# A hybrid decoder block on one core: pace of the attention, order of the loads at the border of the output projection, and its weights asked a unit ahead

## The chip, the core and the metric

The kernel runs on one core of a Trainium2 chip. Five engines work side by side, each through its own queue in order: TensorE (PE in the profile, its weight loads PEld), VectorE (DVE), ScalarE (ACT), GpSimd (POOL) and SyncE (SP, whose queue SPq issues nearly all transfers here; 16 DMA engines carry them out). They wait for one another through semaphores. The metric is the device time of one execution in microseconds (us).

## What is computed

The reference is one layer over x of 2048 positions by 1024 channels:

```python
h = rmsnorm(x, norm1_g[l])
proj = h @ w_in[l]
p_q, p_k, p_v, p_g, p_a, c_b, c_c, c_h = jnp.split(proj, splits, axis=-1)
...
o = gla_chunked(q, k, v, log_a)
o = rmsnorm(o, gla_norm_g[l]).astype(x.dtype)
o = o * jax.nn.silu(p_g.reshape(bsz, seq, GLA_HEADS, GLA_DV))
...
o_conv = c_b * causal_depthwise_conv(u, conv_w[l])
mixed = jnp.concatenate([o_gla, o_conv], axis=-1) @ w_out[l]
x = x + mixed
h2 = rmsnorm(x, norm2_g[l])
ffn = (jax.nn.silu(h2 @ w_ffn_gate[l]) * (h2 @ w_ffn_up[l])) @ w_ffn_down[l]
x = x + ffn
```

and a last RMSNorm. The attention is gated linear attention in chunks with a state that is carried from chunk to chunk; the convolution part takes 512 of the 1024 columns that the output projection mixes.

## The kernel before

**Products.** Every matrix is float32 and is split in two numbers of a shorter format, a high and a low one (`split`, L195: ScalarE rounds to the high part, L198; VectorE subtracts it to get the low part, L199). A product of two tiles is then three matmuls: high by high, high by low, low by high (`product_step`, L496 to L498). The large multiplications are done in units of 2 x 2 blocks by a scheme that needs seven products instead of eight. `PRODUCTS` (L38) lists their operands: weights A11, S1, S2, A12, S3, S4, A22, and inputs B11, T1, T2, B21, T3, B22, T4, in this order. A unit's seven results are added up by VectorE (L530; at the border L1351) or copied out by ScalarE (L542).

**Whole operands and pairs.** Input operands lie in DRAM either as a pair (high and low, 512 KB) or, for T3, B22 and T4 (`WHOLE`, L47), whole (256 KB), so that they have to be split once they are loaded. `load_undivided` loads a whole one, `load_pair` a pair; both take a buffer of the pool `opp`, which has 28. In a unit the whole ones are split when they fall due (`due`, L580): T3 behind the fourth product's sum, and so on.

**Order of work.** The 2048 positions are four blocks of 512, done in two halves of two blocks. Second half's input projection (`in_proj(1, ops)`, L1834) is 12 units: keys and queries, values (units 0 to 3), gate (units 4 and 5, with a silu on ScalarE, L597), convolution (units 6 to 11). Then comes the border: the first half's output projection, `first_out_proj` (L1331), in four units d0 = 0, 2, 4, 6. Each has seven convolution products of six matmuls (operands of `mix_operands`) and 48 matmuls on the attention's heads (L1383, L1389), and each loads 1 MB of `wout` into one of two `raw` buffers. Then `out_proj` (L1421 to L1424) does the second half with plain products, first the convolution's channels, then the heads; the feed-forward part follows.

**Attention in the background.** `gla_half` is a generator whose steps are put between the products. Of three steps to a chunk one does scores (L1170) and transposes (L1176, L1179), one turns the chunk before around (L1245) and asks the next chunk's 14 small loads, and one, the output step, does the outputs (L1195, L1202), the state (L1210), the root mean square of each head (L1227 squares, L204 logarithm, L205 exponential) and the scaled result `osb` (L1236). `tick` (L276) is called after each product; a unit has seven ticks, a unit of the border eight. Every second tick takes one step of the background. While `hasty` holds, the odd tick whose count leaves 3 on division by four takes one too, so three ticks in four; `hastened(steps, n)` sets that and ends it at step n. Other odd ticks advance the making of the convolution operands (`ahead`). In the second input projection the background is a pause of three steps, then `gate(1)` (5 steps) with `gla_half(0)` (27 steps) under `hastened(..., 26)`, and behind it, under `hastened(..., 9)`, `gla_half(1)` of the same length, which runs on into the border.

**Queues.** The order in which each engine gets its instructions is fixed when the program is built, by a list scheduler: of the instructions that it thinks ready, it takes the one first written. So a load or a split can be issued well ahead of its place in the code, once its buffer is thought free. `behind(marks)` (L163) queues what it holds behind the marks on the marks' engine alone: behind a sum it holds back VectorE's half of a split and not ScalarE's.

The functions that the change touches and what calls them:

Of the kernel before, what the change touches and what calls it, by code (L numbers as in the profile page):

```python
# [20 lines left out]
P = 128  # L21
# [33 lines left out]
def tile_hymba_block(ctx, tc, x, xt, win, wa, wgu, wout, wffn, wdown, wdown_first, small, out):  # L55
# [106 lines left out]
    @contextmanager  # L162
    def behind(marks):  # L163

        with ExitStack() as stack:
            for m in marks:
                stack.enter_context(tc.issue_after(m.ins))
            yield
# [134 lines left out]
    def pause(n):  # L303
        for _ in range(n):
            yield

    def hastened(steps, n):
        hasty.append(True)
        for i, _ in enumerate(steps):
            if i == n:  # L310
                hasty.clear()
            yield
# [17 lines left out]
    def no_operands():  # L330
        return {b: [] for _, b in PRODUCTS}
# [88 lines left out]
    def raw_weights(src):  # L420
        n = src.shape[-1]
        raw = rawp.tile([P, 4 * PB], F32, name="raw", tag="raw")[:, 0 : 4 * n]
        raw = raw.rearrange("p (a n) -> p a n", a=4)
        raw_loads.append(load(raw, src))
        return raw
# [154 lines left out]
    def due(n):  # L580
        for o in undivided.pop(n, ()):
            with behind(last_out):
                split(o[:, 1, :].bitcast(F32), o[:, 0, :], o[:, 1, :])
# [398 lines left out]
    def load_undivided(src):  # L982
        o = opp.tile([P, 2, PB], F32R, name="op", tag="op")
        load(o[:, 1, :].bitcast(F32), src[:])
        return o
# [7 lines left out]
    def load_pair(src):  # L993
        o = opp.tile([P, 2, PB], F32R, name="op", tag="op")
        load(o[:].bitcast(F32), src[:])
        return o
# [11 lines left out]
    def gate(half, ops, mark=None):  # L1008

        a = bank("a_ps")
        names = "B11", "T1", "B21", "B22"
        with behind([mark] if mark else []):
            for n in names:
                for k in range(4):
                    q = {"B11": 3 * k + 1, "T1": 3 * k, "B21": 2 * k + 13, "B22": 2 * k + 12}[n]
                    w = wa_sb[:, 32 * q : 32 * q + P]
                    for e in range(2):
                        pe.matmul(  # L1020
                            a[:], w, ops[n][k][:, e, :],
                            start=(n, k, e) == ("B11", 0, 0),
                            stop=n == "B22" and k == 3 and e == 1, skip_group_check=True,
                        )
        if mark:
            yield

        stacks = []
        if half == 0:
            second_factor()  # L1030
        for j in range(2):
            stack = bx[0].tile([96, PB], F32R, name="a_sb", tag="b")
            r, low = [slice(32 * n, 32 * n + 32) for n in (j, 1 - j)]
            with behind(held):
                act.activation(stack[r, :], a[r, :], AF.Copy)
                act.activation(stack[64:96, :], a[r, :], AF.Copy)
                dve.tensor_tensor(stack[low, :], a[r, :], stack[r, :].bitcast(F32), ALU.subtract)
            stacks.append(stack)
        yield
        for j in range(2):  # L1040
            small = decays[2 * half + j] = [
                mtiny.tile([P, 2, PT], F32, name=n, tag=n, bufs=4) for n in ("em", "dn", "el")
            ]
            for i in range(2):
                z = bank("z")
                pe.matmul(
                    z[:], wgu_sb[:, i * P : (i + 1) * P], stacks[j][:], start=True, stop=True
                )
                forget_gate(2 * half + j, i, z, *small)
                yield  # L1050
# [69 lines left out]
    def gla_half(half):  # L1120
        chunks = [(b, t) for b in (2 * half, 2 * half + 1) for t in range(PT)]
        with tc.issue_after(last_silu[0].ins):
            tables = act.preload_act_table_set("natural_log_exp_and_others")
        fetched = gla_fetch(*chunks[0])
        yield
        with tc.issue_after(tables.ins):
            cur = gla_scaled(*fetched)
        yield
        o = None
        for n, (b, t) in enumerate(chunks):  # L1130
            s = gla_scores(b, t, *cur)
            yield
            if n + 1 < len(chunks):
                fetched = gla_fetch(*chunks[n + 1])
            if o is not None:
                yield from gla_finish(*chunks[n - 1], *o)
            o = gla_outputs(b, t, *s)
            if n + 1 < len(chunks):
                cur = gla_scaled(*fetched)
            yield  # L1140
        yield from gla_finish(b, t, *o)
        done.add((b, t))
        yield
# [166 lines left out]
    def mix_operands():  # L1310
        for _ in ahead.pop():
            pass
        s_conv["B22"] = s_mix[1][2:4]
        ops = no_operands()
        for _, n in PRODUCTS:
            ops[n] = [(load_undivided if n in WHOLE else load_pair)(p) for p in s_conv[n]]
            if n in WHOLE:
                undivided[n] = ops[n]
        return ops, [[load_pair(s_gla[j][:, k]) for j in range(2)] for k in range(HEADS)]

    def residual(d0):
# [9 lines left out]
    def first_out_proj(y, conv, heads):  # L1331

        ssq = [
            tiny.tile([P, PB], F32, name=f"ssx{j}", tag=f"ssx{j}", bufs=1) for j in range(2)
        ]
        for d0 in range(0, KD, 2):
            raw = raw_weights(wout[d0 // 2]).rearrange("p a (b e c) -> p (a b) e c", e=2, c=P)
            quads = [raw[:, k : k + 2, e, :] for e, k in ((0, 4), (0, 6), (1, 6), (1, 4))]
            w = unit_weights(None, quads)
            wh = [weight_quarter(raw[:, 0:HEADS, e, :]) for e in range(2)]  # L1340

            def mul(i, o=None):
                first = o is None
                o = bank() if first else o
                n, m = PRODUCTS[i]
                for k in range(2):
                    product_step(o, w[n], conv[m], k, first)
                return o

            def plus(at, o):  # L1350
                summed = dve.tensor_tensor(y[at][:], o[:], y[at][:], ALU.add)  # L1351
                all_plus.append(summed)
                if d0 == 0:
                    last_plus[:] = last_out[:] = [summed]

            oa = mul(0)
            plus((0, 0), oa)
            ob = mul(1)
            plus((1, 1), ob)
            due("T3")  # L1360
            tick()
            mul(2, oa)
            plus((0, 1), oa)
            due("B22")
            o = mul(3)
            tick()
            mul(4, oa)
            plus((1, 1), oa)
            due("T4")
            mul(5, ob)  # L1370
            plus((0, 1), ob)
            tick()
            mul(6, oa)
            plus((1, 0), oa)
            tick()
            following = residual(d0 + 2) if d0 + 2 < KD else None
            for e in range(2):
                po = [bank() if e or j else o for j in range(2)]
                for k in range(HEADS):
                    c = slice(k * P, (k + 1) * P)  # L1380
                    for j in range(2):
                        for part in range(2):
                            pe.matmul(  # L1383
                                po[j][:], wh[e][:, 0, c], heads[k][j][:, part, :],
                                start=k + part == 0 and e + j > 0, stop=False,
                                skip_group_check=True,
                            )
                    for j in range(2):
                        pe.matmul(  # L1389
                            po[j][:], wh[e][:, 1, c], heads[k][j][:, 0, :], start=False,  # L1390
                            stop=k == HEADS - 1, skip_group_check=True,
                        )
                    if k % 2:
                        tick()
                for j in range(2):
                    plus((e, j), po[j])
                    store(s_x1[j][d0 + e][:], y[e, j][:])
                    sum_squares(ssq[j], y[e, j][:], d0 + e == 0)
            y = following
        return ssq  # L1400
# [429 lines left out]
    drain_background()  # L1830
    ops = load_pairs(s_h1)
    ahead.append(conv_operands())
    background.extend([pause(3), hastened(chain(gate(1, ops), gla_half(0)), 26)])
    in_proj(1, ops)  # L1834
    drain_background(lambda: (1, PT - 1) in done)
    ssq = first_out_proj(residual(0), *mix_operands())
# [118 lines left out]
```

## Time and profile before

| what | value |
|---|---|
| median of 3 runs | 2037.68 us (2036.74 to 2039.19) |
| the profiled execution's own time | 2035.8 us |
| its span, first instruction to last | 2034.0 us |
| granted clock of TensorE over the span | 0.997 |
| HBM read, written | 277.60 MB, 145.75 MB |
| DMA, mean over the span | 209 GB/s |

In a row of the timeline stand the start and the duration in us, engine, line, operation, what it writes and reads, and how many instructions are taken together; in brackets how long the engine had been idle and what ended that. Matmuls are pipelined: one of 512 columns shows some 0.39 us, and its successor starts earlier than that. Each row of a table by stage has the stretch and its length, the busy time of PE, PEld, DVE, ACT and POOL with the number of instructions, the granted clock, the busy share of the DMA engines and GB/s.

### The profile page before, as it was taken

The numbers are of one execution on the slowest core, as the hardware profiler recorded it, in microseconds if no ns is written. First come the engines' busy times: TensorE is split into PE (matmuls) and PEld (weight loads), VectorE is DVE, ScalarE is ACT, GpSimd is POOL, SyncE is SP. The second block draws the span as 40 slices with busy tenths as digits, with TensorE's granted clock in tenths as the row PEclk, the third lists the DMA queues.
The fourth block names the chain that finished last, engine by engine and source line by source line (L and its number), as shares of the span: only waits on it lengthen the run. The fifth ranks groups of instructions, "written<-read, shape, count | busy, mean of one in ns | idle before, by whom it ended". The sixth has DMA issues, their size and how long they took to land.

```text
span 2034.0 us, 27037 instructions
## 1 busy us (share of the span) xinstructions
PE 2010.5 (99%) x9275; PEld 1653.5 (81%) x9275; DVE 1566.8 (77%) x2837; ACT 978.3 (48%) x1944; POOL 10.3 (1%) x17
## 2 busy tenths in 40 slices
PE   9999999999999999999999999999999999999998
PEld 8788887778878888888888888887888888888886
DVE  7888868678767877777777688887767767778886
ACT  6664465765543444444444552334434444454345
POOL 0000000000000000000000000000000000000001
PEclk9999999999999999999999999999999999999999
DMA  7356866655596863446545676576444434586653
GB/s 264 120 201 219 289 261 214 192 177 176 183 318 227 281 244 135 182 153 214 181 150 186 225 282 252 185 278 275 167 158 171 169 137 171 179 332 219 248 217 130
DMA packets 193482, 425.16 MB, mean 209 GB/s; under 512 B 20320, under 2 KB 67648, under 8 KB 183872
## 3 DMA queue, kind: packets, MB, share of 16 engines
q1 hardware_dynamic: 192624, 422.77, 58.7%
q8 instruction: 73, 1.20, 0.2%
q10 hardware_dynamic: 720, 0.66, 0.1%
q14 instruction: 65, 0.53, 0.1%
HBM read 277.60 MB, written 145.75 MB: 208 GB/s over the span
## 4 chain that ended last, share of the span: by engine, by line
PE 92%; DMA 3%; DVE 2%; ACT 2%; issue 1%; SPq 1%; POOL 0%; POOLq 0%; ACTq 0%; DVEq 0%
PE mm L496 27%; PE mm L498 27%; PE mm L497 26%; PE mm L1422 1%; PE mm L1424 1%; PE mm L1421 1%; PE mm L1383 1%; DMA op<-shT 1%; PE a_ps L1020 1%; PE mm L801 1%; PE mm L803 1%; PE mm L802 1%; PE mm L1741 1%; PE mm L1389 1%; DMA raw<-in_win_dram 1%
## 5 line engine op out<-in xcount | busy, mean ns | idle before, releaser
L496 PE MATMUL mm<-op,wq 128*128 128x512 f32 x2499 | 973.0, 392 | 5.2 <-DVE osb L1236 2.0
L497 PE MATMUL mm<-op,wq 128*128 128x512 f32 x2499 | 972.2, 390 | 0.3 <-DVE op L199 0.2
L498 PE MATMUL mm<-op,wq 128*128 128x512 f32 x2499 | 962.0, 390 | 2.4 <-DVE wq L199 2.1
L198 ACT ACTIVATE wq<-raw 128x512 fp32r<-128x512 f32 (+2 forms) x628 | 361.2, 581 | 601.0 <-PE mm L498 497.2
L496 PEld LDWEIGHTS mm<-op,wq 128*128 128x128 f32 x2499 | 469.3, 188 | 108.0 <-ACT wq L198 2.9
L498 PEld LDWEIGHTS mm<-op,wq 128*128 128x128 f32 x2499 | 469.3, 188 | 102.5 <-DVE wq L199 4.4
L497 PEld LDWEIGHTS mm<-op,wq 128*128 128x128 f32 x2499 | 469.5, 188 | 98.1 <-DVE op L199 2.0
L199 DVE TENSOR_TENSOR wq<-raw,wq 128x512 fp32r<-128x512 f32 (+2 forms) x628 | 390.5, 627 | 149.3 <-ACT wq L198 147.6
L530 DVE TENSOR_TENSOR c<-mm,c 128x512 f32<-128x512 f32 x196 | 134.9, 688 | 71.5 <-PE mm L498 66.8
L530 DVE TENSOR_TENSOR y<-mm,y 128x512 f32<-128x512 f32 x185 | 126.9, 689 | 53.5 <-PE mm L498 52.9
L542 ACT ACTIVATE c<-mm 128x512 f32<-128x512 f32 x198 | 115.7, 589 | 32.4 <-PE mm L498 29.8
L448 DVE TENSOR_TENSOR raw<-raw 128x512 f32<-128x512 f32 (+2 forms) x190 | 116.8, 621 | 2.1
L198 ACT ACTIVATE wq<-s 128x512 fp32r<-128x512 f32 (+2 forms) x100 | 58.0, 580 | 106.8 <-PE mm L498 93.7
L448 DVE TENSOR_TENSOR s<-raw 128x512 f32<-128x512 f32 (+2 forms) x95 | 59.1, 622 | 33.4 <-DMA raw<-in_wffn_dram 18.0
L199 DVE TENSOR_TENSOR op<-op 128x512 fp32r<-128x512 f32 x108 | 71.2, 686 | 1.8 <-ACT op L198 1.7
L198 ACT ACTIVATE op<-op 128x512 fp32r<-128x512 f32 x108 | 63.1, 621 | 14.2 <-DMA op<-scT 7.0
L199 DVE TENSOR_TENSOR wq<-s,wq 128x512 fp32r<-128x512 f32 (+2 forms) x100 | 62.5, 625 | 1.8 <-ACT wq L198 1.0
L448 DVE TENSOR_TENSOR raw<-s,raw 128x512 f32<-128x512 f32 (+2 forms) x95 | 59.1, 622 | 1.3
L597 ACT ACTIVATE sg<-mm 128x512 f32<-128x512 f32 x26 | 15.6, 598 | 87.6 <-PE mm L498 87.6
L597 ACT ACTIVATE c<-c 128x512 f32<-128x512 f32 x78 | 49.0, 629 | 15.4 <-DVE c L530 12.7
L1421 PE MATMUL mm<-op,wq 128*128 128x512 f32 x128 | 50.2, 392 | 0.0
L1422 PE MATMUL mm<-op,wq 128*128 128x512 f32 x128 | 49.8, 389 | 0.0
(238 smaller groups left out, 1664.5 us busy)
## 6 DMA issues: line engine op xcount, KB each, us to landing
raw<-in_wffn_dram SPq DMA_DIRECT2D x44, 1024.0 KB, 6.4
sa_B<-so SPq DMA_DIRECT2D x47, 512.0 KB, 4.2
op<-sa_B SPq DMA_DIRECT2D x47, 512.0 KB, 6.7
raw<-in_win_dram SPq DMA_DIRECT2D x22, 1024.0 KB, 5.9
sa_T<-so SPq DMA_DIRECT2D x44, 512.0 KB, 4.5
op<-sa_T SPq DMA_DIRECT2D x44, 512.0 KB, 6.4
raw<-in_wdown_dram SPq DMA_DIRECT2D x24, 768.0 KB, 5.4
sx<-y SPq DMA_DIRECT2D x48, 256.0 KB, 4.2
```

The costliest lines, as they stand in the source:

```text
L198: last_hi[:] = [act.activation(hi, src, AF.Copy)]
L199: last_lo[:] = [dve.tensor_tensor(lo, src, hi.bitcast(F32), ALU.subtract)]
L448: dve.tensor_tensor(*args)
L496: pe.matmul(o[:], wh, xh, start=first and k == 0, stop=False, skip_group_check=True)
L497: pe.matmul(o[:], wh, xl, start=False, stop=False, skip_group_check=True)
L498: return pe.matmul(o[:], wl, xh, start=False, stop=k == n - 1, skip_group_check=True)
L530: last_plus[:] = [dve.tensor_tensor(t[:], o[:], t[:], ALU.add)]
L542: last_out[:] = [act.activation(t[:], o[:], AF.Copy)]
L597: last_silu[:] = [act.activation(s[:], c[:], AF.Silu)]
L801: pe.matmul(acc[:], wq[:, 0, c], p[:, 0, :], start=first, stop=False)
L1421: pe.matmul(o[e, j][:], wh, m[:, 0, :], start=n == 0, stop=False)
L1422: pe.matmul(o[e, j][:], wh, m[:, 1, :], start=False, stop=False)
```

## The change

In `mix_operands` the three whole convolution operands (two tiles each) are loaded ahead of the four pairs, and their splits are written there, VectorE's halves behind the last sum of the input projection; the three `due` calls in `first_out_proj` go. In `first_out_proj` the weights of unit d0 + 2 are asked before those of unit d0 are split. And the first attention's hastened stretch ends at step 12 instead of 26.

```diff
         ops = no_operands()
+        for n in WHOLE:
+            ops[n] = [load_undivided(p) for p in s_conv[n]]
         for _, n in PRODUCTS:
-            ops[n] = [(load_undivided if n in WHOLE else load_pair)(p) for p in s_conv[n]]
-            if n in WHOLE:
-                undivided[n] = ops[n]
+            if n not in WHOLE:
+                ops[n] = [load_pair(p) for p in s_conv[n]]
+        with behind(last_plus):
+            for n in WHOLE:
+                for o in ops[n]:
+                    split(o[:, 1, :].bitcast(F32), o[:, 0, :], o[:, 1, :])
         return ops, [[load_pair(s_gla[j][:, k]) for j in range(2)] for k in range(HEADS)]
...
+        raws = raw_weights(wout[0])
         for d0 in range(0, KD, 2):
-            raw = raw_weights(wout[d0 // 2]).rearrange("p a (b e c) -> p (a b) e c", e=2, c=P)
+            raw, raws = raws, raw_weights(wout[d0 // 2 + 1]) if d0 + 2 < KD else None
+            raw = raw.rearrange("p a (b e c) -> p (a b) e c", e=2, c=P)
...
             plus((1, 1), ob)
-            due("T3")
             tick()
             mul(2, oa)
             plus((0, 1), oa)
-            due("B22")
             o = mul(3)
             tick()
             mul(4, oa)
             plus((1, 1), oa)
-            due("T4")
...
-    background.extend([pause(3), hastened(chain(gate(1, ops), gla_half(0)), 26)])
+    background.extend([pause(3), hastened(chain(gate(1, ops), gla_half(0)), 12)])
```

## The prediction

> **What bounds the kernel now.** I read the page first, then a table by stage of the half that the change touches, then the idle times of TensorE in order of time.
>
> ```profile
> span 2034.0 us, 27037 instructions
> PE 2010.5 (99%) x9275; PEld 1653.5 (81%) x9275; DVE 1566.8 (77%) x2837; ACT 978.3 (48%) x1944; POOL 10.3 (1%) x17
> ```
>
> TensorE is busy 2010.5 of 2034.0 us. The change neither adds nor removes a matmul, so it can only win or lose idle time: 23.5 us in the whole kernel, plus what a lower clock costs. The table by stage (stretch, length and then busy time of PE, PEld, DVE, ACT and POOL, granted clock, DMA share, GB/s) shows where. The rows are the two gate units of the second input projection, its other units, and the four units of the first output projection (d0 = 0, 2, 4, 6).
>
> ```profile
> 373.00:420.00 47.00, 43.48 (x259) 34.87 (x259) 29.82 (x65) 39.86 (x75) 0.00 (x0) 1.00 0.59 186
> 420.00:537.00 117.00, 116.84 (x636) 94.65 (x635) 89.58 (x190) 63.74 (x169) 0.00 (x0) 1.00 0.50 157
> 563.00:595.00 32.00, 29.35 (x148) 22.42 (x146) 17.32 (x42) 11.20 (x37) 0.00 (x0) 0.95 0.89 317
> 595.00:619.00 24.00, 22.87 (x112) 18.49 (x112) 21.69 (x51) 14.23 (x39) 0.00 (x0) 1.00 0.80 283
> 619.00:640.00 21.00, 21.00 (x94) 17.41 (x93) 13.73 (x27) 6.31 (x13) 0.00 (x0) 1.00 0.48 162
> 640.00:660.50 20.50, 20.50 (x92) 16.95 (x92) 14.71 (x25) 7.16 (x12) 0.00 (x0) 1.00 0.89 319
> ```
>
> Idle TensorE: 47.00 - 43.48 = 3.5 us in the gate units, 2.65 at d0 = 0, 1.1 at d0 = 2, nothing later. Its rows in order of time name the releaser:
>
> ```profile
> 315.52 0.50 PE L498 MATMUL mm<-op,wq 128*128 128x512 f32 x1 [2.14 <-DVE wq L199]
> 391.54 0.47 PE L496 MATMUL mm<-op,wq 128*128 128x512 f32 x1 [1.67 <-DVE osb L1236]
> 408.64 0.63 PE L1179 MATMUL v_ps<-ident,vt 128*128 128x128 f32 x4 [1.84 <-ACT wq L198]
> 570.25 0.41 PE L1176 MATMUL kt_ps<-ident,kq 128*128 128x128 f32 x2 [2.19 <-ACT wq L198]
> 571.69 0.80 PE L496 MATMUL mm<-op,wq 128*128 128x512 f32 x1 [0.46 <-DVE y L1351]
> 595.38 0.47 PE L496 MATMUL mm<-op,wq 128*128 128x512 f32 x1 [0.28 <-DVE osb L1236]
> 600.67 1.16 PE L1195 MATMUL o_ps<-vt,scores 128*128 128x128 f32 x8 [0.35 <-ACT vt L1181]
> 602.97 0.50 PE L496 MATMUL mm<-op,wq 128*128 128x512 f32 x1 [0.49 <-DVE y L1351]
> ```
>
> The largest is that at the border, 570.25. The timeline of all engines just ahead of it tells its cause:
>
> ```profile
> 560.53 0.38 SPq L152 DMA_DIRECT2D op<-scT  x1
> 561.49 0.38 SPq L152 DMA_DIRECT2D op<-scT  x1
> 565.82 0.63 ACT L198 ACTIVATE op<-op 128x512 fp32r<-128x512 f32 x1 [4.88 <-DMA op<-scT]
> 567.10 0.63 ACT L198 ACTIVATE op<-op 128x512 fp32r<-128x512 f32 x1
> 567.34 0.71 PE L1170 MATMUL sc<-kq 64*128 64x128 f32 x8
> 568.41 0.17 DVE L1230 TENSOR_SCALAR hsq<-hsq 128x4 f32<-128x4 f32 x1 [5.24 <-ACT sq L1227]
> 569.68 0.76 DVE L1236 TENSOR_TENSOR osb<-o_ps,hsq 128x256 f32<-128x256 f32 x2
> ```
>
> The last two whole operands (T4) are asked at 560.53 and 561.49. ScalarE's queue is in order: with the split of T4 at its head it stands 4.88 us until the first has landed. The squares of the attention's outputs stand behind it, so VectorE stands 5.24 us, so the accumulators are emptied late, and TensorE has no free bank until `osb` is made at 569.68 and after. This one late load holds three engines. The clock falls after it; two matmuls ahead of it and two behind it, and the granted clock (last but two column) of the stretch:
>
> ```profile
> 563.17 0.39 PE L498 MATMUL mm<-op,wq 128*128 128x512 f32 x1
> 563.40 0.39 PE L496 MATMUL mm<-op,wq 128*128 128x512 f32 x1
> ...
> 572.28 0.63 PE L497 MATMUL mm<-op,wq 128*128 128x512 f32 x1
> 572.71 0.63 PE L498 MATMUL mm<-op,wq 128*128 128x512 f32 x1
> ```
>
> ```profile
> 570.00:575.00 5.00, 4.29 (x18) 3.29 (x18) 5.00 (x12) 1.55 (x4) 0.00 (x0) 0.66 1.07 395
> ```
>
> Starts are 0.43 us apart instead of 0.23, and 4.29 us of work at 0.66 lose 4.29 x 0.34 = 1.4 us.
>
> **The change part by part.**
>
> *Whole operands first, split early.* The 14 convolution operands take buffers as the last unit of the input projection frees them. T3, B22 and T4 move to the head of the line, so the place at 560.53 falls to a B21 pair. T4 lands well ahead of its split, and the six splits run early. On ScalarE they cost nothing that isn't paid now. VectorE's halves have this row on the page:
>
> ```profile
> L199 DVE TENSOR_TENSOR op<-op 128x512 fp32r<-128x512 f32 x108 | 71.2, 686 | 1.8 <-ACT op L198 1.7
> ```
>
> Six of them, 6 x 0.69 = 4.1 us, go behind the last sum of the input projection into the 5.24 us in which it now stands; if that cover were gone they would delay the first sums by as much. What goes: 2.19 + 0.46 + 1.4 = **4.0 us**. What is late next is B21, wanted by the fourth product instead of the last. TensorE gets there at about 567.34 + 0.71 + 0.41 + 0.63 = 569.1 without the stall (scores, then two groups of transposes). B21 is a pair of 512 KB. These rows (size, time to landing) bound it:
>
> ```profile
> op<-sgla SPq DMA_DIRECT2D x8, 512.0 KB, 8.0
> op<-scB SPq DMA_DIRECT2D x4, 512.0 KB, 5.6
> ```
>
> Asked at 561.49, it is there at 567.1 or 569.5: a wait of 0 to 0.4 us. I take +0.3. A gain below nothing is excluded, as no wait stands in that place now.
>
> *Weights one unit ahead.* The second 1 MB of the output weights is now asked late:
>
> ```profile
> 586.62 0.44 SPq L152 DMA_DIRECT2D raw<-in_wout_dram  x1
> 594.47 0.72 ACT L198 ACTIVATE wq<-raw 128x256 fp32r<-128x256 f32 x2 [4.60 <-DMA raw<-in_wout_dram]
> ```
>
> ScalarE waits 4.60 us for it, and splitting, sums and attention then crowd VectorE at d0 = 2 (21.69 of 24.00 us busy). Asked a unit earlier, the splitting can spread into d0 = 0, where VectorE has 14.7 us free. At stake are the three small waits, 0.28 + 0.35 + 0.49 = 1.1 us; between 0 and that I take **-0.5**, since the attention steps that name two of them stay. The price on the queue is a rival below.
>
> *First attention at one in two.* The count of its steps, worked out from the ticks in the code: it now runs three ticks in four until step 26, in future until step 12. Its later steps spread over the units after the gate, the second attention starts 10 ticks later, and 13 of its steps instead of 8 fall into the border: 4, 4, 4 and 1 at d0 = 0, 2, 4, 6 instead of 4, 4, 0, 0. The first 12 steps are unchanged, so the wait at 315.52 stays. In the gate units ScalarE is the busy one, 39.86 of 47.00 us, and these rows stand just ahead of the wait at 391.54:
>
> ```profile
> 387.19 1.28 ACT L204 ACT_TABLE_LOAD   x1
> 388.71 1.28 ACT L205 ACT_TABLE_LOAD   x1
> 391.12 1.28 ACT L597 ACT_TABLE_LOAD   x1
> ```
>
> Logarithm and exponential of an attention step each load a table, the gate's silu loads its own again: 2.6 us stand ahead of `osb`, and TensorE waits 1.67 of them. At the new pace the gate units hold about two output steps instead of three or four. Two can still stand between two silus, so the waits 1.67 + 1.84 = 3.5 go wholly or not at all; I take half, **-1.8**. The cover for what moves into the units behind is VectorE's 27 us free in 420-537.
>
> At d0 = 4 and 6 VectorE is busy 65% and 72%. With four steps d0 = 4 comes to look like d0 = 2, which lost 1.1 us; d0 = 6, with one step, is left at nothing. Between 0 and 1.1 I take **+0.7**. Attention ends 6 ticks ahead of the border's end, so nothing has to be drained; the next projection takes its convolution parts first, which covers the last chunk's store.
>
> **Sum:** -4.0 + 0.3 - 0.5 - 1.8 + 0.7 = -5.3 us. The profiled execution took 2035.8 us, 1.9 below the median of the runs (2037.7). Its terms apply to the median as well: 2037.7 - 5.3 = **2032.4**. With every bound at its good end: -4.0 - 1.1 - 3.5 = -8.6, 2029.1.
>
> The Trainium skill, TensorE: Matmul & The Clock Gate, "What's actually happening", has the clock halved only after an idle window of about 3.4 us. The row above shows 0.66 after waits of 2.19 and 0.46 us, so here the measurement decides. By the page the 1.4 us would not hang on this wait, and the sum would be -3.9.
>
> **The rivals.**
>
> *Only the border's first wait goes* (chance 0.23). For it: a silu can still stand on each side of an attention step. The gate units keep their waits, d0 = 4 takes its price: -4.0 + 0.3 - 0.3 + 0.7 = -3.3, 2034.4.
>
> *The load is late all the same* (0.15), so that the change doesn't do what it says. The second 1 MB of weights enters the line ahead of B21. The DMA's rows around there:
>
> ```profile
> 550.00:555.00 5.00, 5.00 (x24) 4.09 (x23) 1.45 (x4) 2.77 (x6) 0.00 (x0) 1.00 0.99 356
> 555.00:560.00 5.00, 5.00 (x39) 4.24 (x39) 5.00 (x12) 2.93 (x8) 0.00 (x0) 1.00 0.41 107
> ```
>
> At 356 GB/s 1 MB takes 2.9 us. B21 then costs a wait of 0.4 + 2.9 = 3.3, with the lower clock 4.7: the 4.0 are paid back. With d0 = 4's 0.7 and nothing won elsewhere: +1.4, 2039.1. Against it: the share is 0.41 in 555-560, where the line has room. The Trainium skill, DMA: Bandwidth & Descriptors, "Queues, rings and completion order", has each DMA engine consume its ring in order, which speaks for this rival; the landing times of 8.0 us for 512 KB in the crowded stretch agree.
>
> *The queue itself stands* (0.17, the slower one). SyncE issues in order, and the new weights load must wait for the buffer of the last input weights, whose last reader is the second row here:
>
> ```profile
> 544.76 1.00 SPq L152 DMA_DIRECT2D op<-scB  x2
> 549.15 0.68 DVE L199 TENSOR_TENSOR wq<-raw,wq 128x512 fp32r<-128x512 f32 x1
> ```
>
> If that load stands ahead of the pairs, the queue holds from 544.76 to 549.83, 5.1 us, and 2.9 of transfer follow. B21 comes 0.4 + 8.0 = 8.4 us late; with the clock, and with d0 = 4's price: -4.0 + 8.4 + 1.4 + 0.7 = +6.5, 2044.2. It makes the kernel slower by over 0.2% from a wait of about 6 us on. Against it: the loads of operands come first in the program.
>
> **How the numbers follow.** The forecast has 0.45, with its own range of 2029 to 2033.6. 0.2%, about what a measurement of this kernel can tell from no change, is 4.1 us: under 2033.6 is faster, over 2041.8 slower. The forecast gives faster 0.45; the first two rivals lie within (0.38), the third is slower (0.17). The range 2028.5 to 2042 leaves out most of the third case and little of the first.
>
> **What would show it.** Right: no ScalarE wait on a T4 load and no VectorE wait of 5 us at the border, a granted clock of 1.00 there, the second weights issued before 560 instead of 586.62, T4's low halves made before 565, fewer table loads between the silus. Wrong: TensorE waiting for a load of B21 or of the heads, a gap of several us in SyncE's issues, waits at d0 = 4, or the waits of the gate units unchanged.

## The result and the profile after

The changed kernel is slower by a little: 2043.98 us (median of 11 runs, 2039.32 to 2047.93) beside 2039.24 for the kernel before on the same chip (11 runs), a ratio of 1.0020 with a 95% interval of 1.0012 to 1.0028. That is some 4 us more, where 5.3 less was forecast.

The profiled execution of the changed kernel is the slowest of its runs (2047.93, span 2046.2); that of before was at the fast end (2035.8). So some of the 12 us between the two traces is spread between executions, and I compare stretches rather than totals. The yardstick is the stretch from the product behind the wait at 315 us to the last head product of the border: 1814 matmuls are recorded in it in the trace of every kernel, so a difference there is idle or slow time. From the timeline of TensorE its last row before (the first is that at 315.52 in the prediction):

```profile
660.23 0.62 PE L1389 MATMUL mm<-op,wq 128*128 128x512 f32 x2
```

and its first and last row after:

```profile
316.48 0.50 PE L498 MATMUL mm<-op,wq 128*128 128x512 f32 x1 [2.12 <-DVE wq L199]
669.56 0.62 PE L1393 MATMUL mm<-op,wq 128*128 128x512 f32 x2
```

The start of the second matmul in the last row is 0.23 us behind the row's: 660.46 - 315.52 = 344.94 before, 669.79 - 316.48 = 353.31 after, **8.4 us longer**. The table by stage of the changed kernel, the same stretches as before:

```profile
373.00:420.00 47.00, 47.00 (x254) 38.17 (x253) 29.28 (x64) 36.26 (x72) 0.00 (x0) 1.00 0.57 184
563.00:595.00 32.00, 24.16 (x126) 19.44 (x125) 13.35 (x33) 12.07 (x31) 0.00 (x0) 0.89 0.85 310
595.00:619.00 24.00, 20.32 (x102) 15.80 (x101) 18.52 (x43) 11.30 (x32) 0.00 (x0) 0.86 0.78 238
619.00:640.00 21.00, 21.00 (x118) 17.12 (x116) 15.06 (x35) 8.40 (x24) 0.00 (x0) 1.00 0.56 179
```

The gate units have lost all their waits (47.00 of 47.00). TensorE is further on in the changed kernel, so the rows from 563 on don't hold the same work as before. The border has gained: 7.84 us of idle TensorE in 563-595 instead of 2.65, 3.68 in 595-619 instead of 1.13, and a granted clock of 0.89 and 0.86. The waits of TensorE at the border, from its timeline:

```profile
557.33 0.47 PE L496 MATMUL mm<-op,wq 128*128 128x512 f32 x1 [0.67 <-DVE hsq L212]
559.14 0.50 PE L496 MATMUL mm<-op,wq 128*128 128x512 f32 x1 [0.87 <-DMA op<-scB]
582.04 1.23 PE L1170 MATMUL sc<-kq 64*128 64x128 f32 x8 [7.84 <-DVE kq L1160]
600.24 0.79 PE L496 MATMUL mm<-op,wq 128*128 128x512 f32 x1 [3.68 <-DVE y L1358]
```

The bill adds up about: waits at the border 0.67 + 0.87 + 7.84 + 3.68 = 13.1 against 2.19 + 0.46 + 0.28 + 0.35 + 0.49 = 3.8 before, +9.3; lower clock 24.16 x 0.11 + 20.32 x 0.14 = 5.5 against 29.35 x 0.05 = 1.5, +4.0; gate units -3.5. Together +9.8, for 8.4 measured (busy time and clock are only approximately to be multiplied).

**The 7.84.** The scores wait for scaled keys and queries, these for the exponentials of `ee`, these for loads. SyncE's queue in the changed kernel, without a row left out between the first and the last of these:

```profile
563.63 0.33 SPq L152 DMA_DIRECT2D raw<-in_wout_dram  x1
564.96 0.32 SPq L155 DMA_DIRECT2D sm<-c  x1
566.79 2.27 SPq L152 DMA_DIRECT2D y<-in_xt_dram  x3
569.44 0.33 SPq L155 DMA_DIRECT2D sm<-c  x1
570.62 0.33 SPq L152 DMA_DIRECT2D y<-in_xt_dram  x1
572.44 0.33 SPq L152 DMA_DIRECT2D op<-sm  x1
574.90 2.20 SPq L152 DMA_DIRECT2D kq<-sk  x4
577.47 0.93 SPq L152 DMA_DIRECT2D ee<-sd  x2
```

The rows of ScalarE that use what was loaded, and one of VectorE:

```profile
574.86 0.72 ACT L198 ACTIVATE wq<-raw 128x256 fp32r<-128x256 f32 x2 [4.94 <-DMA raw<-in_wout_dram]
580.67 0.42 ACT L1157 ACTIVATE ee<-ee 128x256 f32<-128x256 f32 x1 [0.64 <-DMA ee<-sd]
...
590.00 3.39 ACT L198 ACTIVATE op<-op 128x512 fp32r<-128x512 f32 x5 [4.63 <-DMA op<-sm]
595.47 0.42 ACT L1157 ACTIVATE ee<-ee 128x256 f32<-128x256 f32 x1 [2.09 <-DMA ee<-sd]
```

```profile
595.92 0.42 DVE L1159 TENSOR_TENSOR kq<-kq,ee 128x256 f32<-128x256 f32 x1 [5.72 <-ACT ee L1157]
```

The 1 MB of weights asked at 563.63 is used from 574.86, 11.2 us later. Between it and the first `kq` load stand seven issues (1 + 3 + 1 + 1 + 1), and the `kq` load is issued at 574.90, as the weights have landed. This is how the queue works throughout this trace: eight transfers are under way at most, and no issue goes out before the one eight places ahead has landed. Heads of 512 KB and 1 MB of weights fill those places, so 64 KB of keys are not even asked before 574.90, and `ee` not before 577.47.

**The 3.68.** ScalarE stands 4.63 us on operands of the next projection (`op<-sm`, 590.00), whose loads and splits the scheduler has drawn up to here, and then 2.09 us on the next chunk's `ee`. VectorE stands 5.72 us for these exponentials, and the sums behind them come late. So ScalarE stands as it did for T4 before, with other data, and the wait that ends last is again one for small loads.

What the change set out to do was done, too. T4 is asked and split early; ScalarE stands 0.17 us for it, and VectorE not at all:

```profile
534.13 1.01 SPq L152 DMA_DIRECT2D op<-scT  x2
```

```profile
542.36 3.69 DVE L199 TENSOR_TENSOR op<-op 128x512 fp32r<-128x512 f32 x6
```

### The profile page after: what moved, and what is told of

Same layout as the page of the kernel before. It is cut to its first block, busy times and chain, and to the rows that moved or that the text cites. A ratio compares the mean times of both kernels' runs of the same rounds, so it can differ in the third digit from the quotient of the medians.

```text
span 2046.2 us, 27013 instructions
## 1 busy us (share of the span) xinstructions
PE 2014.9 (98%) x9275; PEld 1656.8 (81%) x9275; DVE 1566.8 (77%) x2837; ACT 974.9 (48%) x1941; POOL 10.3 (1%) x17
## 3 DMA queue, kind: packets, MB, share of 16 engines
q1 hardware_dynamic: 192624, 422.77, 58.5%
## 4 chain that ended last, share of the span: by engine, by line
PE 95%; DMA 3%; ACT 1%; DVE 1%; issue 0%; SPq 0%; POOL 0%; POOLq 0%; ACTq 0%
PE mm L496 27%; PE mm L498 27%; PE mm L497 27%; PE mm L1426 1%; PE mm L1428 1%; PE mm L1425 1%; PE mm L1387 1%; DMA op<-shT 1%; PE mm L801 1%; PE a_ps L1020 1%; PE mm L803 1%; PE mm L802 1%; PE mm L1745 1%; PE o_ps L1195 1%; PE sc L1170 1%; PE mm L1393 1%
```

## The experiments

All ratios are to the kernel before on the same chip, five rounds each, with 95% intervals; "stretch" is the yardstick above in the one profiled execution (before 344.9). Executions of one kernel lie up to 5 us or more apart, so the ratio decides on the time and the trace on the mechanism. A dip of the clock at its start, which some traces have and others not, is worth some 1.6 us of it (last section). Where an expectation gives theories letters, A has the slower pace as the culprit, B the early weights, C the new order of the loads, and D the attention's small loads behind the heads, by their place in the queue (D1) or by the full line of transfers under way (D2). In the table P is the slower pace, W the whole operands first with early splits, A the weights a unit ahead; L and Q are two edits of mine, shown below.

| label | parts | ratio (interval) | stretch | waits of TensorE at the border over 2 us |
|---|---|---|---|---|
| f_pace | P | 0.9989 (0.9980 to 0.9998) | 347.5 | 3.32 |
| f_whole | W | 1.0009 (1.0000 to 1.0017) | 350.0 | 5.13 |
| f_ahead | A | 0.9995 (0.9986 to 1.0004) | 344.9 | 2.66 |
| f_whole_ahead | W A | 1.0009 (1.0000 to 1.0018) | 348.4 | 4.73 |
| g_pace_whole | P W | 1.0019 (1.0010 to 1.0028) | 349.0 | 8.61 |
| h_pace_ahead | P A | 1.0038 (1.0025 to 1.0050) | 351.0 | 4.45, 5.60 |
| (the change) | P W A | 1.0020 (1.0012 to 1.0028) | 353.3 | 7.84, 3.68 |
| i_late | L | 0.9988 (0.9979 to 0.9997) | 345.5 | 2.05 |
| g_late | W L | 0.9988 (0.9980 to 0.9997) | 344.8 | 2.35 |
| h_pace_ahead_late | P A L | 1.0005 (0.9996 to 1.0014) | 347.9 | 4.46 |
| g_change_late | P W A L | 1.0001 (0.9992 to 1.0010) | 347.1 | 7.41 |
| j_pool | Q | 0.9975 (0.9965 to 0.9984) | 342.4 | 2.18 |
| g_pool | W Q | 0.9991 (0.9982 to 1.0000) | 345.2 | 4.08 |
| i_change_pool | P W A Q | 0.9991 (0.9982 to 1.0000) | 347.0 | 4.64 |
| i_late_pool | L Q | 0.9963 (0.9949 to 0.9977) | 339.2 | none |
| i_pace_late_pool | P L Q | 0.9977 (0.9968 to 0.9985) | 344.6 | 3.37 |
| h_pace_ahead_late_pool | P A L Q | 0.9984 (0.9975 to 0.9993) | 345.2 | 3.39 |
| j_whole_ahead_late_pool | W A L Q | 0.9977 (0.9968 to 0.9986) | 342.2 | none |
| h_change_late_pool | P W A L Q | 0.9995 (0.9986 to 1.0004) | 344.4 | 4.65 |

### The change taken apart

Each part alone is its own hunk of the change. The pace:

```diff
-    background.extend([pause(3), hastened(chain(gate(1, ops), gla_half(0)), 26)])
+    background.extend([pause(3), hastened(chain(gate(1, ops), gla_half(0)), 12)])
```

> Only the attention's pace is changed (hastened to step 12 instead of 26), on the kernel before. Theory A (the small loads of the attention steps that now fall into the border stand behind the operands' traffic in SyncE's queue, and TensorE, whose order is fixed, waits for the scores): the 3.5 us of waits in the gate units go, waits of 5 to 12 us come at the border on scores or on sums behind them, and the time is 3 to 9 us above the kernel before. Theory B (the second weights, asked early, stand in front of these loads): about 3 us below the kernel before, with no such wait at the border. Theory C (the new order of the loads is at fault): also about 3 us below.

The hunks in `mix_operands`, and those that take the three `due` calls away:

```diff
+        for n in WHOLE:
+            ops[n] = [load_undivided(p) for p in s_conv[n]]
...
-            due("T4")
```

> Only the order of the loads and the early splits, on the kernel before. Theories A and B: the wait of ScalarE of about 5 us on T4 and TensorE's 2.2 us behind it go, with the clock's dip; 3 to 5 us below the kernel before, the gate units' waits as before. Theory C: a wait of TensorE for a load of B21 or behind VectorE's six halves takes its place; within 1 us of the kernel before or up to 5 us above it.

The weights:

```diff
+        raws = raw_weights(wout[0])
...
-            raw = raw_weights(wout[d0 // 2]).rearrange("p a (b e c) -> p (a b) e c", e=2, c=P)
+            raw, raws = raws, raw_weights(wout[d0 // 2 + 1]) if d0 + 2 < KD else None
```

> Only the weights asked a unit ahead, on the kernel before. Theory A: the load of the second weights goes out some 20 us earlier than at 586.62, the wait for it at 594 goes; within 1.5 us of the kernel before. Theory B: its 1 MB is in front of the heads or of T4 in the crowded line; 2 to 5 us above the kernel before, with a longer wait of ScalarE for T4 or of TensorE for the heads. Theory C: as A.

And the last two together:

> The change without its pace: new order of the loads, early splits, weights a unit ahead, hastened to step 26 as before. Theory A: faster than the kernel before by 3 to 6 us, and than the whole change by 8 or more; no wait of several us on scores. Theory B: no better than the kernel before, since the weights still stand in the line. Theory C: no better than the kernel before.

No part does alone what the sum forecast. The new load order was to win 4.0 - 0.3 us and is 0.09% slower. Its trace has lost the wait for T4, and has this instead:

```profile
598.10 1.23 PE L1170 MATMUL sc<-kq 64*128 64x128 f32 x8 [5.13 <-DVE kq L1160]
```

So the late load was one of several that were late together; behind it stood the small loads of the next chunk. The pace alone clears the gate units and keeps 0.11% of it, where theory A expected 3 to 9 us more than before; the early weights alone cost nothing, against theory B. So the single parts and the last pair spoke for theory C, the new order. The single parts add up to 0.9993 (-0.11 + 0.09 - 0.05%), the whole is 1.0020: they do not add. I first put that on the new load order meeting the slower pace, and ran the two pairs that were still missing:

> The change without the weights asked ahead: slower pace and new order of the loads. If the two parts' costs add up (-2.2 and +1.9 us by the single runs): within 1.5 us of the kernel before. Theory D (the border has a line of transfers as its bound, and the slower pace puts more attention loads into it just as the early splits let TensorE run up to them): the parts do not add up, 3 to 6 us above the kernel before, as the whole change. If instead the weights asked ahead are what makes the whole change slow together with the pace: within 1.5 us of the kernel before.

> The slower pace and the weights a unit ahead; the operands' load order and splits stay as before. If the loss of the whole change comes from the new load order meeting the slower pace (TensorE runs up to the attention's small loads, which stand behind the heads in SyncE's queue), this pair has no such meeting: the single parts add up, -0.6 and -1.0 us, so 1 to 2 us faster than before (ratio 0.999 to 0.9995), and no wait over 4 us on scores at the border. If the slower pace costs whatever it is put together with, this pair is slower than before by 1 us or more, with a wait on scores of several us.

The first fits; the second refutes it. Pace and early weights without the new order are the slowest of all, 1.0038 (five runs), so theory C is not the whole of it either. The trace shows the same two kinds of wait, scores and sums:

```profile
578.11 1.23 PE L1170 MATMUL sc<-kq 64*128 64x128 f32 x8 [4.45 <-DVE kq L1160]
...
598.23 0.79 PE L496 MATMUL mm<-op,wq 128*128 128x512 f32 x1 [5.60 <-DVE y L1353]
```

What the slowest three share is the pace together with another part of the change. The rows that tell what the pace does to the border are the first sum of the border, the first load of the heads and the first small loads of the second chunk that is scored there. With the slower pace that is an earlier one of the 16 chunks: the last before, the third last in the changed kernel. Before (the timelines of VectorE and SyncE, and from TensorE's the scores that use these loads):

```profile
570.95 0.68 DVE L1351 TENSOR_TENSOR y<-mm,y 128x512 f32<-128x512 f32 x1
```

```profile
561.96 1.29 SPq L152 DMA_DIRECT2D op<-sgla  x2
...
573.03 2.03 SPq L152 DMA_DIRECT2D kq<-sk  x3
```

```profile
593.58 0.71 PE L1170 MATMUL sc<-kq 64*128 64x128 f32 x8
```

and in the changed kernel:

```profile
556.18 0.68 DVE L1358 TENSOR_TENSOR y<-mm,y 128x512 f32<-128x512 f32 x1
```

```profile
552.48 0.59 SPq L152 DMA_DIRECT2D op<-sgla  x1
```

TensorE reaches the border 14.8 us earlier, the heads are asked 9.5 us earlier, and the small loads at that place (574.90, above) 1.9 us later. Before, they were asked 20.6 us ahead of their scores (593.58); now the scores were due at 582.04 - 7.84 = 574.20, ahead of the request. TensorE has come forward, and the queue has not.

### The next projection's loads held back (L)

The eight convolution loads of the next projection (256 KB each, 2 MB; where an expectation says 4 MB it is wrong) wait for the last store of the border's second unit:

```diff
-    all_plus = []
+    all_plus, border_out = [], []
...
-                    store(s_x1[j][d0 + e][:], y[e, j][:])
+                    border_out.append(store(s_x1[j][d0 + e][:], y[e, j][:]))
...
-            with behind(all_plus[-4:-3] if k < HEADS + 2 else all_plus[-2:-1]):
+            with behind((all_plus[-4:-3] if k < HEADS + 2 else all_plus[-2:-1]) + [border_out[-9]]):
```

> As f_whole, with the eight loads of the next projection's convolution operands (2 MB, of which six go out at 583 to 599 in f_whole) held back until the second unit of the border has stored its results. Theory D2: with 1.5 MB less in the crowded stretch the attention's loads land about 3.5 us earlier, the wait on the scores falls from 5.1 to 2 us or less, and the time is 2 to 4 us below f_whole. Theory D1: six places less in the queue, so about the same. Theory E (only the fixed order of TensorE, not the line, makes the wait): within 1 us of f_whole.

> The whole change, with the eight loads of the next projection's convolution operands held back as in g_late. Theory D2: ScalarE's wait of 4.6 us for such a load at 590 and a part of the 7.8 us on the scores go; 3 to 7 us below the whole change, so about at the kernel before or 2 us below. Theory D1 or E: the second wait, 3.7 us behind the load that ScalarE stands on, still goes, as ScalarE's order holds it; the first stays; 2 to 4 us below the whole change.

> The pair without the new load order, and the next projection's eight convolution loads held back until the second border unit has stored its results. If the line of transfers bounds the border, taking 4 MB out of its crowded stretch wins here as it did with the new load order alone (3.7 us) and with the whole change (4.5 us), less where the border waits less: 2 to 4 us below the pair, so 3 to 6 us faster than before (ratio 0.997 to 0.9985). If holding back only mends what the new load order spoils, it gives nothing here: the same as the pair within 1 us.

> The kernel before with the next projection's convolution loads held back, nothing else. If those loads are late guests of a line that is full at the border in every version, holding them back wins 1 to 3 us here too, as it won 3.7 us with the new load order and 4.5 us with the whole change. If it mends only what the change spoils, the time stays within 1 us of before.

The edit wins in these four companies: 0.12% on the kernel before, 0.21% on W, 0.19% on the whole change, 0.33% on P A. So it doesn't only mend something that the change spoilt. Where the small loads are on another queue as well (next section), its worth can't be told: 0.9975 to 0.9963 on the kernel before, intervals that overlap, and 0.9991 to 0.9995 on the whole change. P A with it is 6.7 us below P A, where 2 to 4 were expected, and still no faster than before. On W the wait on scores falls from 5.13 to 2.35, about as theory D2 had it. In the whole change it takes away the second wait (3.68) and leaves the first:

```profile
581.29 1.23 PE L1170 MATMUL sc<-kq 64*128 64x128 f32 x8 [7.41 <-DVE kq L1160]
```

### The small loads on another queue (Q)

The attention's 14 loads per chunk, 64 KB each, are issued by GpSimd instead of SyncE:

```diff
-                load(dst[:, i, :], r[:, s])
+                pool.dma_start(dst[:, i, :], r[:, s])
```

> New order of the loads and early splits, as in f_whole, and the small loads of all attention steps issued from GpSimd's queue instead of SyncE's. Theory D1 (these loads are late because they stand behind heads, residuals and weights in SyncE's queue, which holds at each issue until a transfer eight places ahead has landed): they go out several us earlier, the wait of 5.1 us on the scores at 598 goes or shrinks under 2 us, and the time is 3 to 5 us below f_whole, so 1 to 3 us below the kernel before. Theory D2 (the DMA engines are full, so that whatever is asked lands late): the loads go out earlier and land 8 us or more after, the wait stays at 3 us or more, and the time is that of f_whole within 1.5 us. If GpSimd issues slowly, above 1 us each, it is slower everywhere and tells nothing.

> The whole change with one edit, the attention's small loads on GpSimd's queue; nothing is held back. If their place in SyncE's queue is what cost the whole change its 4.7 us, the 7.8 us wait on scores at 582 falls under 3 us and the time comes back to before within 1.5 us (about 2039), though the next projection's loads still share the line. If the full DMA engines make them late from any queue, the wait stays over 5 us and the time at about 2043.

> The kernel before with one edit: the attention's small loads on GpSimd's queue. With the loads of the next projection held back as well it was 0.37% faster than before, with those held back alone 0.12%. If place in SyncE's queue is the border's main price already before the change (T4's load at 560.53 stands behind the small loads too), this edit alone gives the difference: 4 to 6 us faster, and T4 is asked before 556 with no TensorE wait over 1 us for it. If the two edits need each other, it gives under 2 us and the wait at the border stays.

On the whole change it takes 0.29% off (1.0020 to 0.9991, intervals apart), and the wait at 582 is gone. The loads of that chunk are asked at 552.43, as soon as the matmuls that read their buffers are over (`o_ps`, L1202), instead of 574.90; they take longer to land (5.3 to 6.0 us for `kq`, 3.4 to 4.7 in the changed kernel), and their scores start at 583.07 without a wait. So it is the place in SyncE's queue that made that wait, and not the landing. Another wait of 4.64 us on scores appears further ahead. From the timelines of GpSimd, VectorE, ScalarE and TensorE in i_change_pool, and the table by stage:

```profile
526.79 2.11 POOL L1153 DMA_DIRECT2D kq<-sk  x4 [6.60 <-DMA sgla<-gt]
...
552.43 2.11 POOL L1153 DMA_DIRECT2D kq<-sk  x4 [18.27 <-PE o_ps L1202]
```

```profile
545.30 3.69 DVE L199 TENSOR_TENSOR op<-op 128x512 fp32r<-128x512 f32 x6
```

```profile
559.08 0.40 ACT L1157 ACTIVATE ee<-ee 128x256 f32<-128x256 f32 x1
```

```profile
560.52 1.22 PE L1170 MATMUL sc<-kq 64*128 64x128 f32 x8 [4.64 <-DVE kq L1160]
```

```profile
545.00:560.00 15.00, 10.71 (x62) 8.38 (x60) 14.93 (x37) 5.81 (x22) 5.28 (x10) 1.00 1.02 392
```

This is no wait for loads. The scores at 560.52 use those asked from 526.79 on, of which `kq` and `ee` had landed by 531.7 (the loads of 552.43 are the next chunk's, whose `ee` land after the exponentials of 559.08 have begun). What is late is VectorE, busy 14.93 of 15.00 us, with the six early splits at the head of the stretch; the exponentials and the scaled keys stand behind its work. The same wait, on the same chunk, is 4.65 in h_change_late_pool, and 3.37 and 3.39 in i_pace_late_pool and h_pace_ahead_late_pool, which have the slower pace without the early splits. All four have the pace.

On W (g_pool) the time falls by 0.18%, 3.7 us as theory D1 had it, but a wait of 4.08 us stays. It isn't one for loads either: they are asked at 560.28 instead of 587.74 (f_whole) and have landed by 568.5, and the scores start at 595.34. The exponentials (592.93) stand in ScalarE's order behind the squares of the unit's sums (591.80, L1268).

On the kernel before, the same line of code is worth 0.25% (5.1 us of 2038.3, where 4 to 6 were expected). It also tells where the late T4 came from. SyncE's queue before, ahead of the T4 loads at 560.53 and 561.49:

```profile
548.74 3.69 SPq L152 DMA_DIRECT2D kq<-sk  x4
552.78 1.00 SPq L152 DMA_DIRECT2D ee<-sd  x2
554.15 1.98 SPq L152 DMA_DIRECT2D vt<-sv  x4
556.17 2.83 SPq L152 DMA_DIRECT2D gt<-sg  x4
```

and with the small loads elsewhere (j_pool):

```profile
554.91 0.83 SPq L152 DMA_DIRECT2D op<-scT  x2
```

The 14 small loads held the queue from 548.74 to 559.00, 10.3 us for 0.9 MB. Without them both T4 loads are asked from 554.91 on, and TensorE doesn't wait for T4 at all, with the old load order. It does wait there for the other two whole operands. ScalarE stands 4.32 us for T3 (`op<-scT`) and 0.66 + 1.37 us for B22 (`op<-sm`), VectorE 4.62 us behind it, and TensorE behind a sum; the first and the last of these rows:

```profile
555.38 1.35 ACT L198 ACTIVATE op<-op 128x512 fp32r<-128x512 f32 x2 [4.32 <-DMA op<-scT]
...
562.72 0.50 PE L496 MATMUL mm<-op,wq 128*128 128x512 f32 x1 [2.18 <-DVE c L530]
```

All in all TensorE is idle 3.76 us in 537-619 here, and 3.78 before. In these two traces what the edit wins lies elsewhere: idle gate units 1.3 us instead of 3.5, and a clock of 1.00 instead of 0.95 in 563-595. One execution each can't settle how the 5.1 us divide.

### Both edits, with and without the parts of the change

> The whole change, the next projection's convolution loads held back, and the attention's small loads (14 to a chunk) issued by GpSimd's queue instead of SyncE's. With the loads held back alone, TensorE still waited 7.4 us on scores at 581. If the place behind the heads and weights in SyncE's queue makes these small loads late, the wait falls under 2 us and the kernel comes 3 to 5 us below its sister without this edit, to about 2035. If they are late because the DMA engines are full, whatever queue they are issued from, the wait stays above 4 us and the time within 1 us of 2039.

> The same two edits (loads held back, small loads on GpSimd's queue) on the pair without the new load order. T4 is then late as before (a wait of about 2 us of TensorE at the border is expected), but the scores are not. If the new load order is worth its 4 us once the small loads come in time, as the prediction priced it, this kernel is 3 to 4 us slower than its sister with the whole change. If the order is worth nothing because what follows is late anyway, the two agree within 1 us.

> The kernel before with the next projection's convolution loads held back and the attention's small loads on GpSimd's queue; pace, load order and weights as before. It prices the two edits alone. If they mend only what the slower pace brings, this kernel is within 1 us of before. If they relieve the border whatever the pace, it is 1 to 3 us faster, and the sister with the slower pace and weights ahead (3.3 us faster than before) owes its gain to them.

> The slower pace alone, on the same two edits. If the slower pace is worth its gate-unit waits (3.5 us) once the border's small loads come in time, this kernel is 2 to 4 us faster than the one with the two edits alone, and no wait on scores at the border is over 5 us. If the five attention steps that it moves to the border cost as much as the gate units gain, the two agree within 1 us.

> The two relieving edits with the new load order and the weights a unit ahead, but with the old pace: the whole change but for the slower pace. If the loss comes with the pace, it stays within 1.5 us of the two edits alone (0.9963 of before) and 2 to 5 us below the whole change with the same two edits (0.9995). If the new load order costs in the relieved border too, it stands half-way or higher, at 0.998 or more.

The two edits alone beat both kernels: 2032.47 us (5 runs, 2030.88 to 2036.05) beside 2040.67, ratio 0.9963. Their gate units and border, by stage:

```profile
373.00:420.00 47.00, 45.69 (x271) 36.83 (x270) 34.08 (x78) 39.29 (x84) 20.10 (x39) 1.00 0.63 206
...
563.00:595.00 32.00, 30.97 (x165) 24.16 (x164) 29.01 (x71) 15.12 (x46) 5.28 (x10) 1.00 0.85 309
595.00:619.00 24.00, 24.00 (x119) 19.71 (x119) 18.23 (x38) 9.50 (x25) 0.00 (x0) 1.00 0.51 165
```

TensorE is idle 1.0 us at the border, where it was 3.8 before, at a full clock. No part of the change that is added to this makes it faster: W A 0.9977, P 0.9977, P A 0.9984, P W A 0.9995; of these only the last has its interval apart from that of the two edits alone. The new order wins nothing here: h_pace_ahead_late_pool, without it, is not slower than h_change_late_pool, with it, where 3 to 4 us were expected. That doesn't price T4's own wait, since with the small loads elsewhere T4 is not late without the new order either. In h_change_late_pool the wait on scores did not fall under 2 us as expected; it is the one behind VectorE told above. I had expected the pace to be worth 2 to 4 us on the two edits; it isn't. It costs about 2.8 us (0.9963 to 0.9977, intervals that overlap; 0.9977 to 0.9995 with W A, on different chips, points the same way). j_whole_ahead_late_pool, all but the pace, lies between what its two theories had: 2.9 us above the two edits alone (1.5 at most if the loss were the pace's) and 3.7 below the whole change with them. So the pace is a part of the loss, and whether the rest is the new order's is not shown. The trace of i_pace_late_pool, taken of the slowest of its runs (2039.38), has no wait left in the gate units, but this:

```profile
558.01 1.22 PE L1170 MATMUL sc<-kq 64*128 64x128 f32 x8 [3.37 <-DVE kq L1160]
```

```profile
550.00:560.00 10.00, 5.72 (x36) 4.35 (x33) 8.33 (x25) 5.63 (x21) 5.28 (x10) 0.84 1.02 386
560.00:570.00 10.00, 10.00 (x41) 7.99 (x40) 5.99 (x11) 2.98 (x7) 0.81 (x2) 0.82 1.05 393
```

The loads of this chunk were asked at 526.45, so it waits behind VectorE (7.60 of 8.00 us busy in 550-558), where an attention step meets the last unit's work and the first products of the border: 4.28 us idle in 550-560, and 5.72 x 0.16 + 10.00 x 0.18 = 2.7 us of clock. The two edits had taken most of the gate units' waits without it (45.69 of 47.00 us are busy), so the pace had 1.3 us left to win.

## Why the prediction was wrong, point by point

*Which step failed.* "What is late next is B21". B21 was late next, by 0.87 us (0 to 0.4 forecast, 0.3 taken), but what came after it was later: the small loads of a chunk (7.84), and then the operands of the next projection and the next chunk's small loads (3.68). I asked what is late behind T4 in the order of the products. I should have asked it in the order of SyncE's queue.

*The whole operands first, -4.0 + 0.3.* The mechanism did what it was said to do: T4's two waits at 570 and 571 are gone, and in the changed kernel the splits run at 542.36. The price was wrong. Alone the part is 1.0009, for the 4.0 us came back as a wait on scores of 5.13. The row that I took for the cause, T4 asked at 560.53, was itself an effect: it stood behind 14 small loads for 10.3 us, in rows of the trace of before that I did not read. What was put beside it as a condition, that VectorE's splits cost where their cover is gone, shows with the small loads on another queue: 4.65 us with them (h_change_late_pool), 3.39 without (h_pace_ahead_late_pool), one trace each.

*The weights a unit ahead, -0.5.* They are issued at 563.63 instead of 586.62, not before 560 as said, and ScalarE still waits 4.94 us for them. Alone 0.9995, which can't be told from nothing and doesn't speak against -0.5. But they take 11.2 us to land there, and the small loads stand behind them.

*The pace, -1.8 + 0.7.* The gate units lost 3.5 us of waits, all that stood there, where half was forecast. Behind 600.24 TensorE has no wait left at the border, so d0 = 4 costs nothing instead of 0.7. The count of steps, four each at d0 = 0 and 2 as before, made me price nothing there. A count of steps is not enough: the loads of the two chunks scored at the border had 18.6 and 20.6 us of lead in the trace of before, and that lead was what the earlier border used up. Had the loads of each step been set against the queue's order, the sign would have been in doubt.

*The rivals.* "The queue itself stands" had the sign and, by chance, the size (2044.2). Its place was another: not the weights' buffer ahead of the pairs, but eight transfers under way, with heads and weights among them. B21 was not 8.4 us late; the small loads were. "The load is late all the same" is refuted by T4's early splits, and "only the border's first wait goes" by the gate units.

The Trainium skill, DMA: Bandwidth & Descriptors, "Queues, rings and completion order", was drawn on for a rival: each DMA engine consumes a ring in order. The trace agrees: what SyncE's queue has issued lands in the order of issue in the traces of before and after. In j_pool, where the two kinds stand in different queues, small loads pass large ones: a head of 512 KB asked at 556.14 took 10.3 us, and keys asked at 560.50 took 5.0, so they landed ahead of it.

*What stays open.* Why P A (1.0038) is slower than P W A (1.0020), with intervals that touch: both have the same two waits, and one trace each doesn't tell. How the pace's price on the two edits divides between the wait on scores and the clock behind it, of which there is one execution. And what the new load order and the early splits each cost: no run has the one without the other.

## What to carry to other kernels

A load that lands late is often late because of what stands ahead of it in its queue: read the issuing queue back from the late load until it is no longer busy, and move what is small and urgent out from behind what is large, before reordering the loads themselves. When steps of a background are moved, count the loads that each issues and where they fall in the queue, not the steps. And where one wait ends, price the next thing in that queue, and then the next in the order of the engines themselves; two parts that clear the same wait don't add (Q alone 0.9975, with W 0.9991).

## What the runs showed of the hardware that I had not expected

The same wait can leave the clock alone or not. Ahead of 316 us TensorE waits 2.14 us in the kernel before and 2.10 in f_pace, with the same work; the table by stage gives a granted clock of 1.00 in the one and 0.72 in the other. Before:

```profile
315.00:321.00 6.00, 5.48 (x28) 4.67 (x28) 6.00 (x16) 2.78 (x9) 0.00 (x0) 1.00 0.59 185
```

f_pace:

```profile
315.00:321.00 6.00, 5.61 (x18) 4.46 (x19) 5.38 (x14) 1.55 (x7) 0.00 (x0) 0.72 0.62 191
```

At 0.72 over 5.61 us that is 1.6 us. In f_pace the matmuls from 316.25 to 319.60 start 0.43 us apart instead of 0.23, and then run at full speed again. All twenty traces have this wait, of 2.1 to 2.4 us: the clock of 315-321 is 1.00 in ten of them and 0.72 or 0.73 in the other ten, whatever the parts. So it can be a part of the spread between executions.

The same small loads are cut differently by the two queues. The DMA part of the page before, and of j_pool:

```profile
q1 hardware_dynamic: 192624, 422.77, 58.7%
```

```profile
q1 hardware_dynamic: 160368, 408.08, 56.3%
q0 software_dynamic: 7168, 14.69, 2.5%
```

From SyncE 14.69 MB went in 192624 - 160368 = 32256 packets of some 455 bytes, from GpSimd in 7168 of 2049. Their share of the DMA engines was about the same (2.4 and 2.5%).
